# Two buffer pools in the mixer, weight sums beside the output projection, and sixteen shared feed-forward blocks instead of ten

## The chip, the core and the metric

The kernel runs on one core of one Trainium2 chip. The metric is the device time of one execution in microseconds (us). Engines are named as in the profile: PE is TensorE's matmul, PEld its weight load, DVE is VectorE, ACT is ScalarE, POOL is GpSimd, SP is SyncE, which issues nearly all transfers here.

## What is computed

One layer of a hybrid decoder on 1024 tokens of 1024 channels, all in float32. Cut to what matters here:

```python
h = rms_norm(x, norm_pre_mix)
mix = hybrid_mixer(h, ...)            # RWKV-7 heads and a causal convolution, 31 wide; then @ w_out
x = x + rms_norm(mix, norm_post_mix)
h = rms_norm(x, norm_pre_ffn)
hid = causal_dwconv(h @ ffn_up, ffn_conv_w, ffn_conv_b)   # 1024 x 5632, convolution 3 wide
gate, up = hid[..., :2816], hid[..., 2816:]
x = x + rms_norm((gelu(gate) * up) @ ffn_down, norm_post_ffn)
```

## The kernel before

**Numbers.** Each float32 operand of a large matmul is split into a high part, rounded to the matmul's format, and the rest; three matmuls (high x high, high x low, low x high) stand for one product. A weight is loaded raw (`weight`, L164), its high part is cast by ACT and its low part subtracted by POOL (`split`, L159). There are two buffers each for the parts ("wh", "wl") and three for the raw weight ("wr").

**Halves and blocks.** Tokens are worked on in two halves of 512, h0 and h1. The up projection has 22 blocks of 128 channels, each with a gate branch and an up branch. `ffn_pair` (L901) computes a block for one half: for each of two branches 8 k-tiles x 3 = 24 matmuls of 512 columns into one PSUM bank, then `taps` (L883), the convolution of three taps: one ACT pass and two DVE passes that read the bank. The product with the gelu of the gate follows on DVE.

**Plain and shared blocks.** A plain block is a pair for h0 and a pair for h1: 96 matmuls. A shared block is computed for both halves and both branches together, by Winograd's form of Strassen's product for a 2 x 2 split: seven products of 12 matmuls. Two of them need h0 alone (`gates`, L939: the first of them is copied aside as "firsts", the sum of both goes through the taps as the gate), five follow in `shared` (L1004), so 24 + 60 = 84 matmuls. The five need sums of the activations, made once (`act_sums`, L962, 3 steps for each of four k on ACT and DVE), and sums of the block's weights, made by POOL (`four_sums`, L1054, four subtractions of 128x512). The down projection (`ffn_down`, L1103) is seven such products over 11 blocks each, and sums of its weights are made ahead and kept in DRAM: `weight_sums` (L1068) has twelve steps (11 for ffn_down, one for the first shared block), each with four loads, `four_sums` and four stores.

**Numbers of blocks.** EARLY = 12 (L53), JOINT = 10 (L55), PLAIN = 22 - 10 = 12.

**Order.** The mixer works in four quarters of 256 tokens; the recurrence goes through chunks of 64. At its end (`mixer`, L1386 and on) twelve pairs of h0 (blocks 0 to 11) fill TensorE beside the last recurrence and convolution, in two "pb" banks; their results go to DRAM (`early`). Then comes the output projection of the second half (`w_out`, L763: 16 weights, 384 matmuls of 256 columns), whose six-deep weight buffers are the tags "ca" and "ck". After it `run` (L1201) opens the pools of the feed-forward part: all of the mixer's buffers lie in one pool, `mix`, that ends with it. The ten gate blocks (12 to 21) follow; `side` (L915, `beside`) puts steps of the second half's norm and then of the weight sums beside them. Then twelve pairs of h1 (blocks 0 to 11) with one step of the weight sums and one or two of `act_sums` each, then the ten shared blocks, then the down projection. From the gates on, the up projection has six banks in turn (xs, pe, pb, two each).

Instructions of an engine run in a fixed order, which the compiler's scheduler makes from priorities and its own model of time; `high_priority` and `issue_after` bend it.

## Time and profile before

| | |
|---|---|
| median of 3 runs | 1273.73 us (1272.41 to 1276.63) |
| the profiled execution | 1273.13 us |
| its span, first to last instruction | 1271.4 us |
| PE, DVE, ACT, POOL busy | 96%, 70%, 58%, 39% |
| DMA | 146 GB/s over the span, 185.7 MB |

The page has the busy time of each engine, the span in 40 slices and the chain of waits; the trace behind it can be asked for stretches, lines and tiles. The spacing of matmuls that follow each other, and not the time that one takes from start to end, says what PE can do. Stages of this kernel, by the first matmuls that belong to them: mixer to about 668 us, output projection of the second half and gate blocks to 777, pairs of h1 to 911, shared blocks to 1054, down projection to the end.

### The profile page before, as it was taken

To read this page: it belongs to the slowest core of one execution; us is meant where nothing else is said; L and a number is where in the kernel's file an instruction comes from. 1 tells how busy PE (TensorE), PEld (TensorE's weight loads), DVE (VectorE), ACT (ScalarE), POOL (GpSimd) and SP (SyncE) were. 2 spreads that over 40 slices of the span, in tenths; PEclk is the share of its full clock that TensorE was granted. 3 is DMA by queue.
4 is the path that set the end of the run, shared out by engine and by line. 5 is a ranking of instruction groups with operands and counts; after the bars stand their busy time and mean duration, and the time that the engine had idled before them with its cause. 6 is when DMAs were issued, how large, how long until landed. Compare 5 with 4: busy or idle time off the path is not lost.

```text
span 1271.4 us, 23025 instructions
## 1 busy us (share of the span) xinstructions
PE 1220.3 (96%) x8460; PEld 990.1 (78%) x8460; DVE 891.2 (70%) x1540; ACT 731.1 (58%) x1518; POOL 495.4 (39%) x438
## 2 busy tenths in 40 slices
PE   6999989999999988999999999999999999999996
PEld 4767767787778877788789878778877888888885
DVE  5286998998679989997631165666356779479667
ACT  7563563655845766566744277776555556545451
POOL 4343320011113332344455369898588860000001
PEclk9999998999999999999999999999999999999999
DMA  7644342343343451232345398888522236336523
GB/s 242 173 133 141 117 134 75 94 134 124 110 135 86 122 183 66 85 84 84 101 132 166 112 336 299 292 305 268 173 65 73 79 127 222 99 98 194 173 76 133
DMA packets 105505, 185.70 MB, mean 146 GB/s; under 512 B 15184, under 2 KB 21712, under 8 KB 105392
## 3 DMA queue, kind: packets, MB, share of 16 engines
q1 hardware_dynamic: 105392, 184.23, 46.2%
q8 instruction: 67, 1.10, 0.4%
q14 instruction: 46, 0.38, 0.1%
HBM read 141.58 MB, written 42.60 MB: 145 GB/s over the span
## 4 chain that ended last, share of the span: by engine, by line
PE 55%; DVE 8%; DMA 3%; POOL 3%; issue 2%; ACT 2%; SPq 0%; POOLq 0%; DVEq 0%; ACTq 0%
PE pb L135 26%; PE pe L135 13%; PE xs L135 11%; PE Y L135 2%; DVE pc L416 2%; PE pc L135 2%; POOL wl L162 1%; DVE nrow L1116 1%; DVE x L1100 1%; POOL b L1056 1%; PE pc L150 1%; DMA pt<-mixd 1%; DMA m<-mixd 1%; PE pe L150 0%; DMA b<-ffn_down 0%
## 5 line engine op out<-in xcount | busy, mean ns | idle before, releaser
L162 POOL TENSOR_TENSOR wl<-wr,wh 128x512 fp32r<-128x512 f32 (+1 forms) x181 | 237.2, 1312 | 247.7 <-ACT wh L162 221.0
L162 ACT CAST wh<-wr 128x512 fp32r<-128x512 f32 (+1 forms) x220 | 135.5, 616 | 170.7 <-issue 43.9
L135 PE MATMUL pb<-h,wh 128*128 128x512 f32 (+3 forms) x720 | 229.5, 398 | 2.5 <-ACT wh L162 1.0
L135 PE MATMUL pb<-f,wh 128*128 128x512 f32 x696 | 219.0, 395 | 2.6 <-ACT wh L162 1.5
L416 DVE SCALAR_TENSOR_TENSOR pc<-c,params,pc 128x512 f32<-128x512 f32 x232 | 174.1, 750 | 8.8 <-ACT pc L413 4.8
L135 PEld LDWEIGHTS pb<-h,wh 128*128 128x128 f32 (+2 forms) x720 | 131.8, 188 | 34.9 <-ACT wh L162 2.6
L135 PEld LDWEIGHTS pb<-f,wh 128*128 128x128 f32 x696 | 130.0, 189 | 31.0 <-ACT wh L162 2.8
L135 PE MATMUL pb<-h,wl 128*128 128x512 f32 (+3 forms) x360 | 146.4, 407 | 2.3 <-POOL wl L162 2.1
L135 PE MATMUL pb<-f,wl 128*128 128x512 f32 x348 | 137.9, 397 | 1.5 <-POOL wl L162 1.5
L157 POOL TENSOR_TENSOR ss<-var,mhalf 128x1 f32<-128x1 f32 x16 | 11.0, 692 | 222.6 <-DVE ss L1097 198.2
L1056 POOL TENSOR_TENSOR b<-b,b 128x512 f32<-128x512 f32 x66 | 86.8, 1317 | 2.8 <-issue 0.9
L135 PE MATMUL pe<-f,wh 128*128 128x512 f32 x272 | 84.2, 391 | 0.1
L135 PEld LDWEIGHTS pb<-h,wl 128*128 128x128 f32 (+2 forms) x360 | 67.7, 188 | 20.7 <-POOL wl L162 4.5
L135 PEld LDWEIGHTS pb<-f,wl 128*128 128x128 f32 x348 | 65.7, 189 | 16.9 <-POOL wl L162 3.1
L135 PE MATMUL xs<-f,wh 128*128 128x512 f32 x200 | 62.0, 391 | 0.4 <-DVE act L953 0.4
L135 PEld LDWEIGHTS pe<-f,wh 128*128 128x128 f32 x272 | 50.9, 188 | 10.6 <-ACT wh L162 0.3
L899 DVE SCALAR_TENSOR_TENSOR pt<-pb,params,pt 128x511 f32<-128x511 f32 (+1 forms) x48 | 35.7, 743 | 30.0 <-ACT ecarry L892 29.5
L162 POOL TENSOR_TENSOR wl<-b,wh 128x512 fp32r<-128x512 f32 x36 | 47.0, 1307 | 21.7 <-ACT wh L162 19.8
L135 PE MATMUL pe<-f,wl 128*128 128x512 f32 x136 | 53.7, 395 | 0.7 <-POOL wl L162 0.7
L706 POOL TENSOR_TENSOR XG<-r,GE 64x256 f32<-64x256 f32 x30 | 20.4, 683 | 86.9 <-DVE r L725 82.0
L178 ACT CAST wh<-wr 128x512 fp32r<-128x512 f32 (+2 forms) x44 | 26.5, 604 | 43.1 <-PE pb L135 31.2
L162 ACT CAST wh<-b 128x512 fp32r<-128x512 f32 x36 | 22.2, 617 | 46.8 <-PE pb L135 18.9
(428 smaller groups left out, 2883.7 us busy)
## 6 DMA issues: line engine op xcount, KB each, us to landing
wr<-ffn_up SPq DMA_DIRECT2D x117, 256.0 KB, 2.8
wr<-w_in SPq DMA_DIRECT2D x80, 256.0 KB, 2.9
b<-ffn_down SPq DMA_DIRECT2D x44, 256.0 KB, 4.4
sums<-b SPq DMA_DIRECT2D x44, 256.0 KB, 4.0
wr<-sums SPq DMA_DIRECT2D x44, 256.0 KB, 2.7
lows<-wl SPq DMA_DIRECT2D x40, 256.0 KB, 3.3
wl<-lows SPq DMA_DIRECT2D x40, 256.0 KB, 2.7
b<-ffn_up SPq DMA_DIRECT2D x40, 256.0 KB, 2.7
```

The source lines that it names most:

```text
L135: return self.nc.tensor.matmul(out, lhsT, rhs, start=start, stop=stop, skip_group_check=skip)
L150: self.nc.tensor.transpose(out, in_, self.con("ident")[:n, :n])
L157: self.nc.gpsimd.tensor_tensor(out, v[:, :n], self.mhalf[:, :n], ALU.pow)
L162: return self.nc.scalar.copy(hi, src), eng.tensor_tensor(lo, src, hi.bitcast(F32), ALU.subtract)
L178: self.nc.scalar.copy(hi, raw)
L416: nc.vector.scalar_tensor_tensor(out, c[:, j:j + HALF], w(j), acc, ALU.mult, ALU.add)
L706: nc.gpsimd.tensor_tensor(x[64:128], R[64:128, gs], w.GE[64:128, c, gs].unsqueeze(2).broadcast_to([64, 4, CH]), ALU.mult)
L899: nc.vector.scalar_tensor_tensor(acc[:, o:], ps[:, :HALF - o], w(j), acc[:, o:], ALU.mult, ALU.add)
L1056: sub = lambda o, x, y, op=ALU.subtract: self.nc.gpsimd.tensor_tensor(o, x, y, op)
L1100: nc.vector.scalar_tensor_tensor(x, f[c], s[:, 1:2], x, ALU.mult, ALU.add)
L1116: nc.vector.tensor_tensor(out, a, b, op)
```

## The change

JOINT becomes 16, so PLAIN is 6. EARLY stays 12: blocks 0 to 5 are plain, 6 to 11 (AHEAD = 6) are shared blocks whose gate is computed in the mixer, 12 to 21 shared blocks whose gate is computed in the gate loop as before.

- In the mixer `ahead` takes the place of `ffn_pair`: six iterations, each with the pair of plain block n and the gate of shared block 6 + n. The gate's bank takes 12 matmuls, is copied aside by ACT, waits for branch 0 of the pair (24 matmuls), takes 12 more; then comes branch 1. "firsts" and the gate go to DRAM.
- The mixer's buffers with tags l8, pt, ck, t2 and po, which the output projection uses, move to a pool of their own, `mixw`; its weights take "pt" and "ck". The feed-forward pools are put into another order, so that those that take the place of the first pool come first, and the activations' pool is cut in two (`ap`, `aq`).
- Five steps of the weight sums are put behind the 2nd, 5th, 8th, 11th and 14th weight of the output projection. With six pairs of h1, the sums are beside four of them and `act_sums` has three or two steps beside each.
- The shared blocks run in the order 6, 7, 12 to 21, 8 to 11. The gates of 6 to 11 come back from DRAM; the results of blocks 6 and 7 are stored to DRAM and come back at the end with the plain ones. `ORDER` permutes the rows of the down projection's weights to match.

```diff
-JOINT = 10
+JOINT = 16
 PLAIN = FT - JOINT
+AHEAD = EARLY - PLAIN
+STORED = 2
+ORDER = [*range(EARLY, FT), PLAIN + STORED, *range(PLAIN, PLAIN + STORED), *range(PLAIN), *range(PLAIN + STORED + 1, EARLY)]
...
+        return (self.mixw if tag in LONG else self.mix).tile(shape, dt, tag=tag, bufs=BUFS[tag], name=self.nm(tag))
...
-                wh, wl = self.weight(self.a["w_out"][ch, k2], [P, 2, 256], (self.mix, "ca", "ck") if h else None)
+                wh, wl = self.weight(self.a["w_out"][ch, k2], [P, 2, 256], (self.mixw, "pt", "ck") if h else None)
+                self.marks.append((self.load, self.low))
...
+        self.tp = pool("tp", 8)
         self.nrowp = pool("nrowp")
-        self.ap = pool("actp", 2 * JOINT)
+        self.ap = pool("actp", 15)
+        self.f2p = pool("f2p", 6)
         self.h1p = pool("h1p", 2 * KT)
-        self.tp = pool("tp", 8)
-        self.f2p = pool("f2p", 6)
+        self.aq = pool("actq", 13)
...
+    def ahead(self, hs, n, row, temp, out):
+        nc = self.nc
+        i = PLAIN + n
+        first, gate = row[:, :HALF], row[:, HALF:]
+        accs = [temp() for _ in range(2)]
+
+        def branch(br):
+            ps = self.project(self.a["ffn_up"][br * FT + n], P, hs)
+            self.taps(0, n, br, ps, accs[br])
+
+        ps = self.bank()
+        self.four(ps, self.weight(self.a["ffn_up"][i, 0], [P, 4, P]), hs[:4], True, True)
+        with self.tc.high_priority():
+            nc.scalar.copy(first, ps)
+        nc.sync.dma_start(self.firsts[n], first)
+        branch(0)
+        self.four(ps, self.weight(self.a["ffn_up"][i, 1], [P, 4, P]), hs[4:], False, True)
+        self.taps(0, i, 0, ps, gate)
+        nc.scalar.activation(gate, gate, AF.Gelu_apprx_tanh)
+        nc.sync.dma_start(self.early[i], gate)
+        branch(1)
+        nc.scalar.activation(accs[0], accs[0], AF.Gelu_apprx_tanh)
+        nc.vector.tensor_tensor(out, accs[0], accs[1], ALU.mult)
+        nc.sync.dma_start(self.early[n], out)
...
-        for n, i in enumerate(range(PLAIN, FT)):
+        for n, i in enumerate(range(EARLY, FT)):
             ps = self.bank()
...
-                late.append(self.weight(B(1, 1)(HT - HELD + len(late)), [P, 512], held=self.hp))
+                home = self.hp if len(late) < HELD - 1 else self.aq
+                late.append(self.weight(B(1, 1)(HT - HELD + len(late)), [P, 512], held=home))
...
-            one = [self.ffn_pair(0, h0, i, temp, act()) for i in range(EARLY, PLAIN)]
-            both = [[act() for _ in range(JOINT)] for _ in range(2)]
+            both = [[act(self.ap if h or n < 5 else self.aq) for n in range(FT - EARLY)] for h in range(2)]
+            for load, low in self.marks[17::3]:
+                with tc.issue_after(load.ins), tc.issue_after(low.ins):
+                    next(sums)
...
-                self.beside(sums, *[ss] * (2 if i % 3 == 0 else 1))
+                self.beside(*[sums] * (i % 3 < 2), *[ss] * (3 if i < 2 else 2))
...
+            pairs = [fetch(n) for n in range(AHEAD - STORED)]
+            order = [*range(STORED), *range(AHEAD, JOINT), *range(STORED, AHEAD)]
+            for m, n in enumerate(order):
+                two = pairs[n] if n < AHEAD else (both[0][n - AHEAD], both[1][n - AHEAD])
+                self.shared(PLAIN + n, S, h1[4:], *two, raws[m % 2 * 4:m % 2 * 4 + 4] if m else None)
+                if n < STORED:
+                    for h in range(2):
+                        nc.sync.dma_start(self.stored[h, n], two[h])
+                    pairs.append(fetch(AHEAD - STORED + n))
...
+            acts = [both[h] + [pairs[STORED][h]] + back[h] + [pairs[n][h] for n in range(STORED + 1, AHEAD)] for h in range(2)]
...
-            for i in range(EARLY):
-                if i % 2 == 0:
+            for n in range(PLAIN):
+                if n % 2 == 0:
                     two = self.row("row", 4)
-                nc.sync.dma_start(self.early[i], self.ffn_pair(0, h0, i, piece, two[:, i % 2 * HALF:(i % 2 + 1) * HALF]))
+                self.ahead(h0, n, self.row("row", 4), piece, two[:, n % 2 * HALF:(n % 2 + 1) * HALF])
```

## Rows read from the trace of the kernel before

**Rows 1.** Page: span; then busy share in tenths in 40 equal slices.

```profile
span 1271.4 us, 23025 instructions
...
PE   6999989999999988999999999999999999999996
...
DVE  5286998998679989997631165666356779479667
...
PEclk9999998999999999999999999999999999999999
```

**Rows 2.** Windows: stretch, length, busy us (instructions) by engine, granted clock, DMA share, GB/s.

```profile
497.60:632.00 134.40, 133.02 (x1234) 106.68 (x1234) 114.63 (x186) 83.15 (x173) 58.03 (x48) 0.99 0.29 85
632.00:668.30 36.30, 35.44 (x157) 29.22 (x157) 12.56 (x17) 17.50 (x35) 20.34 (x16) 1.00 0.45 126
668.30:725.50 57.20, 56.96 (x432) 54.80 (x430) 7.89 (x11) 18.28 (x49) 24.78 (x20) 1.00 0.46 135
725.50:776.70 51.20, 49.15 (x225) 39.12 (x226) 34.09 (x61) 36.82 (x84) 35.46 (x30) 1.00 0.90 313
776.70:905.00 128.30, 126.85 (x551) 102.20 (x550) 72.86 (x108) 91.14 (x193) 107.30 (x85) 1.00 0.80 269
911.00:1054.00 143.00, 141.29 (x611) 112.95 (x610) 92.80 (x134) 79.82 (x166) 111.61 (x85) 1.00 0.34 105
```

**Rows 3.** Chain that ended last, pieces: start us, us, engine, tile, line, count.

```profile
730.33 6.90 DMA m<-mixd
...
900.31 10.88 PE pb L135 x48
...
923.78 2.54 POOL b L1056 x2
```

**Rows 4.** Windows, filling matmuls alone (operand f): length, PE busy (count), PEld, DVE, ACT.

```profile
497.60:632.00 134.40, 106.19 (x422) 77.94 (x422) 0.86 (x2) 0.10 (x1) 0.99 0.29 85
632.00:668.30 36.30, 35.39 (x155) 28.83 (x154) 0.00 (x0) 0.00 (x0) 1.00 0.45 126
```

**Rows 5.** Timeline, two branches' last matmul and taps: start us, us, engine, line, operation.

```profile
574.50 0.39 PE L135 MATMUL pb<-f,wl 128*128 128x512 f32 x1
...
579.79 0.73 DVE L899 SCALAR_TENSOR_TENSOR pt<-pb,params,pt 128x510 f32<-128x510 f32 x1
...
651.54 0.39 PE L135 MATMUL pb<-f,wl 128*128 128x512 f32 x1
...
653.17 1.53 DVE L899 SCALAR_TENSOR_TENSOR pt<-pb,params,pt 128x511 f32<-128x511 f32 x2 [3.18 <-ACT ecarry L892]
```

**Rows 6.** Timeline, DVE: the last splits of the convolution's result.

```profile
629.36 2.50 DVE L162 TENSOR_TENSOR l<-co,l 128x512 fp32r<-128x512 f32 x4 [0.56 <-ACT l L162]
```

**Rows 7.** Lines of ACT, 776 to 905: count, busy us, mean ns, idle before.

```profile
L162 ACT CAST wh<-wr 128x512 fp32r<-128x512 f32 x46 | 28.6, 622 | 29.5 <-PE xs L135 7.0 <-PE pb L135 5.7 <-issue 5.0
L896 ACT ACTIVATE acc<-ecarry,acc,params 128x1 f32<-128x1 f32 x66 | 21.8, 384 | 0.3
L890 ACT ACTIVATE acc<-pe,params 128x512 f32<-128x512 f32 x8 | 6.2, 780 | 0.0
...
L910 ACT ACTIVATE xs<-acc 128x512 f32<-128x512 f32 x5 | 3.0, 601 | 0.3 <-DVE acc L899 0.3
L977 ACT COPY Y<-f 128x512 f32<-128x512 f32 x4 | 2.4, 590 | 0.0
```

**Rows 8.** Lines of POOL: 660 to 725.6 (wm, wl), then 776 to 905 (b).

```profile
L162 POOL TENSOR_TENSOR wm<-wr,wm 128x512 fp32r<-128x512 f32 x16 | 20.7, 1292 | 13.6 <-ACT wm L162 12.7 <-PE pb L135 0.6
L162 POOL TENSOR_TENSOR wl<-wr,wh 128x512 fp32r<-128x512 f32 x8 | 10.4, 1302 | 14.6 <-ACT wh L162 14.6
...
L1056 POOL TENSOR_TENSOR b<-b,b 128x512 f32<-128x512 f32 x39 | 50.5, 1294 | 1.9 <-issue 0.9
```

**Rows 9.** Windows of 10 us: a stretch of the tail, clock third from the end.

```profile
510.00:520.00 10.00, 9.95 (x185) 7.84 (x179) 9.79 (x15) 6.09 (x10) 3.49 (x3) 0.83 0.12 41
```

**Rows 10.** Windows of 10 us: a stretch of the norm, DMA share and GB/s last.

```profile
730.00:740.00 10.00, 10.00 (x46) 8.25 (x45) 7.12 (x12) 5.07 (x12) 3.58 (x4) 1.00 0.99 354
```

More of the change, by code (lines that the diff above doesn't have):

```diff
@@ L105, in __init__ @@
         self.low_pool = True
+        self.tags = {}
+        self.marks = []
     def nm(self, s):
@@ L123, in tl @@
     def tl(self, tag, shape, dt=F32):
-        return self.mix.tile(shape, dt, tag=tag, bufs=BUFS[tag], name=self.nm(tag))
+        return (self.mixw if tag in LONG else self.mix).tile(shape, dt, tag=tag, bufs=BUFS[tag], name=self.nm(tag))
     def par(self, name, j, n=P):
@@ L167, in weight @@
         with self.tc.high_priority():
-            raw = (self.f2p.tile(shape, F32, tag="f2", name=self.nm("wr")) if held is self.hp else
+            raw = (self.f2p.tile(shape, F32, tag="f2", name=self.nm("wr")) if held and held is not self.h1p else
                    self.wp.tile(shape, F32, tag="wr", bufs=3, name=self.nm("wr")))
@@ L207, in setup @@
         self.early = self.dp.tile([EARLY, P, HALF], F32, name="early")
+        self.firsts = self.dp.tile([AHEAD, P, HALF], F32, name="firsts")
+        self.stored = self.dp.tile([2, STORED, P, HALF], F32, name="stored")
         self.x1d = self.dp.tile([SEQ, D], F32, name="x1d")
@@ L220, in setup_mixer @@
         self.mix = pool("mix")
+        self.mixw = pool("mixw")
         self.banks = {"pb": 2, "pc": 1, "pe": 2}
@@ L281, in pair @@
     def pair(self, what, pool):
-        return tuple(pool.tile([P, HALF], F32R, tag="h", name=self.nm(what)) for _ in range(2))
+        return tuple(pool.tile([P, HALF], F32R, tag=self.tags.get(pool, "h"), name=self.nm(what)) for _ in range(2))
     def pairs(self, what, pool=None):
@@ L1070, in weight_sums @@
         nc, a = self.nc, self.a
-        work = [(lambda r, c, j=j: a["ffn_down"][c, r * HT + j], lambda n, j=j: self.sums[n - 1, j]) for j in range(HT)]
+        work = [(lambda r, c, j=j: a["ffn_down"][c, ORDER[r * HT + j]], lambda n, j=j: self.sums[n - 1, j]) for j in range(HT)]
         work.insert(2, (lambda r, c: a["ffn_up"][c * FT + PLAIN, r].rearrange("p k m -> p (k m)"),
@@ L1107, in ffn_down @@
         A11, A12, A21, A22 = acts[0][:HT], acts[0][HT:], acts[1][:HT], acts[1][HT:]
[L1108 removed]
+        B = lambda r, c: lambda j: self.a["ffn_down"][c, ORDER[r * HT + j]]
         T = lambda n: lambda j: self.sums[n - 1, j]
@@ L1207, in run @@
             h0 = self.mixer(sts)
+        tc = self.tc
         with ExitStack() as ctx:
@@ L1229, in run, with fetch @@
             raws = [self.h1p.tile([P, HALF], F32, tag="h", name=self.nm("b")) for _ in range(8)]
-            for n, i in enumerate(range(PLAIN, FT)):
-                self.shared(i, S, h1[4:], both[0][n], both[1][n], raws[n % 2 * 4:n % 2 * 4 + 4] if n else None)
-            kept = []
-            for i in range(0, 8, 2):
-                two = self.row("row", 4)
-                nc.sync.dma_start(two.rearrange("p (i t) -> p i t", i=2), self.early[i:i + 2].rearrange("i p t -> p i t"))
-                kept += [two[:, :HALF], two[:, HALF:]]
-            back = [self.hp.tile([P, HALF], F32, tag="h", name=self.nm("act")) for _ in range(2 * KT)]
-            for i in range(8, EARLY):
-                nc.sync.dma_start(back[PLAIN + i - 8], self.early[i])
-            for i in range(PLAIN):
-                nc.sync.dma_start(back[i], self.plain[i])
-            acts = [kept + back[PLAIN:] + one + both[0], back[:PLAIN] + both[1]]
+            def fetch(n):
+                pair = act(), act()
+                nc.sync.dma_start(pair[0], self.early[PLAIN + n])
+                nc.sync.dma_start(pair[1], self.firsts[n])
+                return pair
+            pairs = [fetch(n) for n in range(AHEAD - STORED)]
[7 more added lines that the diff above has]
+                    pairs.append(fetch(AHEAD - STORED + n))
+            back = [[self.hp.tile([P, HALF], F32, tag="h", name=self.nm("act")) for _ in range(STORED + PLAIN)] for _ in range(2)]
+            for k in range(STORED + PLAIN):
+                for h in range(2):
+                    src = self.stored[h, k] if k < STORED else (self.plain if h else self.early)[k - STORED]
+                    nc.sync.dma_start(back[h][k], src)
+            acts = [both[h] + [pairs[STORED][h]] + back[h] + [pairs[n][h] for n in range(STORED + 1, AHEAD)] for h in range(2)]
             self.ffn_down(acts)
```

5 lines of the change are left out of this document (3 added, 2 removed).

## Prediction

> **What bounds the kernel now.** I read the page first: TensorE is busy nearly everywhere and at the high granted clock in almost every slice, while VectorE is full only in the first half [rows 1]. A mean over stages with different limits says little of a change in some of them, so next I cut the span into the six stages that the edit touches and set the time of each against its matmul work [rows 2]. The unit for that comes from the chain of waits, where 48 matmuls of 512 columns follow each other in 10.88 us [rows 3], that is 0.2267 us each (the "mean ns of one" of a matmul is its latency, not its spacing).
>
> Stage by stage, with the stretches of [rows 2]:
> - 497.6 to 632 (tail of the mixer, feed-forward pairs as filling). 422 filling matmuls [rows 4] are 422 x 0.2267 = 95.7 us of 134.4. The other 38.7 us are the recurrence's and the convolution's small matmuls and the bubbles between them. VectorE is busy 114.6 of 134.4: it and the chain of the recurrence set this pace. The convolution's last split ends at 629.36 + 2.50 = 631.9 [rows 6].
> - 632 to 668.3 is nothing but the rest of the filling: 155 matmuls, 35.1 of 36.3 us [rows 4]. TensorE alone bounds it; VectorE does 12.6 us.
> - 668.3 to 725.5, output projection with the first gate blocks in between: PE 57.0 of 57.2.
> - 725.5 to 776.7, rest of the gate blocks and the norm of the second half: PE idles 2.0 us (51.2 - 49.15), DMA at 0.90; the chain goes here through a 6.9 us load of the norm [rows 3].
> - 776.7 to 911, twelve pairs of the second half: 576 x 0.2267 = 130.6 us of 134.3, 3.7 lost, POOL at 107.3 of 128.3 to 905.
> - 911 to 1054, ten shared blocks: 600 x 0.2267 = 136.0 of 143, 7 lost, most of it in one place at 923 where POOL's weight sums of the second block are late [rows 3].
>
> So from 632 on TensorE is the bound, and a matmul taken away there is time taken away; before 632 it is so only as far as others don't set the pace.
>
> **The change, part by part.** The sum is made against the profiled execution, 1273.1 us (span 1271.4); the median shown is 1273.7, 0.6 more.
>
> (1) Matmuls. A plain block costs 48 for each half, 96; a shared one 24 (gate) + 60 = 84. Six blocks change sides: 6 x 12 = 72 matmuls fewer, 72 x 0.2267 = **-16.3 us**. But they come off as three terms at different places. In the mixer 6 x 72 = 432 instead of 12 x 48 = 576: -144, -32.6 us. In the second half's pairs 6 instead of 12: -288, -65.3 us. In the shared blocks 16 instead of 10: +360, +81.6 us. The 240 of the gate loop stay.
>
> (2) Is the -32.6 us of the mixer really to be had? Up to 632 the old order got 422 filling matmuls done; the new one needs 432 in all. The old rest of 36.3 us shrinks to ten matmuls, 2.3 us, if the filling runs at the old rate. VectorE's share doesn't grow (per iteration three tap pairs and one product for 72 matmuls against two and one for 48), ACT's copies of the first sums (0.6 us, six) and POOL's splits neither. What gets worse is the bank rhythm. In the mixer the filling has two "pb" banks. Before, 24 matmuls on the other bank lie between a branch's end and the next use of its bank, 5.44 us. In `ahead` the gate block holds one bank across branch(0), so branch(1), and the next branch(0), find only 12 in between: 2.72 us. The lag from a branch's last matmul to the end of its second tap is 579.79 + 0.73 - 574.89 = 5.6 us where VectorE is full and 653.17 + 1.53 - 651.93 = 2.8 us where it is free [rows 5]. There are 12 such places. If nothing else is put into the gap, they cost 12 x (5.6 - 2.7) = 35 us at the one and 1 us at the other. But 38.7 us of other PE work has to go somewhere in this stage, 3.2 us for each place, about the 2.9 us that is missing. So most of the wait is not new time. I take **+4 us**, between 0 and +20 (a gain is excluded: less than no wait there is not). Behind the waiting matmuls stand, in PE's order, those of the recurrence, for which VectorE and ACT then wait.
>
> A rule of the skill speaks against this part. The rows show the granted clock at 1.00 from 668 on, where six banks are in turn [rows 2], and 0.83, part of it at the lower level, in a ten-microsecond stretch of the tail, where two are and PE was just filling gaps between small matmuls [rows 9]. The Trainium skill, "TensorE: Matmul & The Clock Gate", section "A second HAM failure mode: psum-queue depth-cycling", says that cycling through banks with small idles between the groups makes the clock fall and rise again. By the rows the sum gets nothing for it; by the rule it would be a rival, (E) below.
>
> (3) Weight sums at the output projection. Five of the twelve sums (marks 17, 20, 23, 26, 29) now run there: each four loads and four stores of 256 KB on SP, and four POOL operations of 1.294 us, 5.2 us [rows 8]. That is 25.9 us of POOL and 10.5 MB. POOL has there 16 splits of w_out and 8 of gate blocks, 20.7 + 10.4 = 31.1 us [rows 8]; together 57.0 of the 57.2 us that PE takes. So POOL is just not the bound, as long as its order lets the splits go first. DMA moves 135 GB/s there [rows 2]; 10.5 MB over 57.2 us are 184 more, 319, under the 354 GB/s that the trace reached [rows 10]. In return the next stage, with DMA at 0.90 and the norm's loads on the chain, has fewer sums to load, and its buffers are there before the output projection ends. On SP the stores of a sum wait for POOL, and queued behind them are the loads of w_out and later of the norm. Bounds: -4 (the 2.0 us idle and the wait for the norm's load go) to +6 us (one SP wait like the 6.9 us load of [rows 3], not hidden). I take **0**.
>
> (4) Six instead of twelve pairs for the second half, with the same act_sums beside. Here ACT is the thing to count. A pair costs it 4 casts x 0.622 + 2 x 0.780 + 6 one-column activations x 0.384 + one gelu 0.601 = 6.95 us; act_sums are 11 operations for each of four k at about 0.59, 26 us [rows 7]. Before: 12 x 6.95 + 26 = 109 us under 130.6 us of PE. After: 6 x 6.95 + 26 = 67.7 us under 65.3. ACT becomes the bound of this stage by 2.4 us, and a cast of a weight then comes late, with POOL's split and 12 matmuls behind it. POOL gets easier: 6 x 4 x 1.29 + 4 sums x 5.2 = 52 us. The stage lost 3.7 us before and should lose about 5 now: **+1.5 us**, bounds -2 (no loss beyond the 2.4 us of ACT) to +7 (ACT's surplus and one more wait like that at 923 in a row).
>
> (5) Six more shared blocks beyond their matmuls. The loss at 923 is at the entry, and stays: the raw weights' buffers come free only after the last pair. The rest of the stage lost about 3 us in nine blocks, 0.3 a block: with the two blocks that are stored and the fetches by SP, **+1.2 us**, bounds 0 to +4.
>
> (6) Down projection: the activations that come back from DRAM are now needed from its third product on, no more from its first; the held weights' buffers come free one by one in the fifth product. PE is saturated there, and nothing shown waits: 0. New stores and loads of "firsts" (6 and 6, 256 KB) and "stored" (4 and 4) are 5.2 MB among 185.7: 0, hidden under the shared blocks, where DMA is at 0.34 [rows 2].
>
> Sum: -16.3 + 4 + 0 + 1.5 + 1.2 = -9.6 us; 1273.1 - 9.6 = 1263.5, with the 0.6 between profile and median **1264 us**.
>
> **The rivals.**
> (A) the forecast, 1258 to 1270.
> (B) All of the matmul term and some of the old losses too: bank waits hidden entirely (0), stage 725.5 to 776.7 and the pairs at their lower bounds (-4, -2), +0.6: -21.7, near 1252; I put 1253 for it. For it: a lighter DMA load just where the norm is on the chain. Against: ACT in the pairs.
> (C) The gain is eaten after 668: POOL at 57.0 of 57.2 and ACT at 67.7 of 65.3 each turn into waits at their upper bounds (+6, +7), with +4 for the banks: -16.3 + 4 + 6 + 7 + 1.2 = +1.9, with half of the two bounds 1269; call it 1272 (1270 to 1277). For it: both counts are at their limit. Against: weights are asked for with high priority, and six of w_out's fit ahead.
> (D) Slower: the bank wait in `ahead`. If the recurrence's matmuls don't fall into the gaps (PE's order is fixed beforehand, and the lag on the chip is what VectorE makes of it), each of the places pays lag - 2.72. The other terms are -13.6, so it is slower by over 3.8 us from 17.4 / 12 + 2.72 = 4.2 us of mean unhidden lag on; the rows have 5.6 and 2.8. With the larger lag at eight of the twelve, before VectorE gets free, 8 x 2.9 = 23 us: 1273.7 - 13.6 + 23 = 1283. Against: 3.2 us of other PE work for each place.
> (E) The clock falls with the bank waits. A ten-microsecond stretch at 0.83 loses 1.7 us; at each of the 12 places that is 20 us, on top of (A) 1284. Only one stretch of the tail shows it so far. The Trainium skill's section named above is what speaks for it.
> (F) The change doesn't do what it says: the new buffers, though in a pool of their own, wait for something that ends late (the last of the mixer's tiles, or SP's queue), and the sums slip behind the output projection. Then ten of them meet six pairs: POOL 6 x 4 x 1.29 + 10 x 5.2 = 83 us under 65.3, +17.7, less the 5 already counted in part: near 1278.
>
> **How the numbers follow.** A measurement of this kernel can tell a change of about 0.3%, 3.8 us, from none; so faster is under 1269.9, slower over 1277.5. Chances: A 0.46, B 0.17, C 0.16, D 0.12, E 0.02, F 0.07. Faster: B and nearly all of A, 0.62. Within: C, a little of A and half of F, 0.21. Slower: D, E and half of F, 0.17. The likeliest is A, 1264 us. The range must leave out no more than 0.2: it starts at 1251, where some of B is still below, and ends at 1279, which leaves out most of D and E.
>
> **What would show it.** The output projection starts near 636 instead of 666 if (2) holds, and the count of filling matmuls before 632 is over 400; PE then waits for VectorE's taps in the tail by less than 5 us in all. Under (D) the output projection starts after 650 and the waits of PE for the taps add up to over 15 us. POOL between 636 and 695 over 90% busy with sums and no wait of PE for it over 2 us supports (3); under (F) no sum operation is seen before the output projection's end. In the pairs ACT over 90% busy and PE losing about 5 us supports (4). Sixteen shared blocks at 13.6 to 13.9 us each support (5). The prediction is wrong if the tail's end moves by less than 20 us, or if a stage between the output projection and the first shared block loses over 8 us more than now.

## The result, and where the time came from

The changed kernel takes 1280.61 us (median of 12 runs, 1275.76 to 1284.39) against 1274.97 for the kernel before on the same chip: a ratio of 1.0047, 95% interval 1.003 to 1.0063. It was forecast to be 10 us faster, and is 6 us slower. Its profiled execution took 1279.6 us with a span of 1277.8, 6.4 more than the span before.

The page of the changed kernel, the rows that answer [rows 1]:

```profile
span 1277.8 us, 22909 instructions
...
PE   5989989999999989999999999989999999999996
...
PEclk8999998999999999999999899999999999999998
```

Nothing stands out at this scale, except some clock digits of 8 where the kernel before has 9, one of them in the middle of the span (703 to 735 us). So the stages again, as windows from one stage's first matmul to the next one's (columns as in [rows 2]): the mixer's tail up to the convolution's last split, the rest of the filling, the output projection, the gates up to the norm's last transpose, the pairs, the shared blocks.

```profile
497.20:634.40 137.20, 133.96 (x1232) 106.81 (x1233) 111.04 (x183) 84.69 (x178) 56.46 (x48) 0.99 0.33 99
634.40:640.20 5.80, 3.27 (x14) 2.05 (x12) 2.05 (x4) 4.12 (x9) 1.16 (x1) 1.00 0.77 238
640.20:694.80 54.60, 53.92 (x410) 52.51 (x411) 8.02 (x12) 17.72 (x47) 48.05 (x38) 0.97 0.93 304
694.80:754.20 59.40, 56.52 (x250) 45.47 (x249) 32.52 (x57) 37.95 (x84) 36.79 (x33) 0.94 0.82 278
754.20:826.90 72.70, 67.40 (x290) 53.34 (x289) 46.52 (x73) 54.84 (x116) 56.23 (x45) 1.00 0.81 273
826.90:1058.20 231.30, 225.01 (x962) 178.84 (x961) 149.01 (x219) 126.04 (x266) 183.59 (x140) 0.99 0.31 93
```

Read at the same first matmuls, before and after (us; output projection and gates as one, because gate matmuls lie in both):

| stage | before | forecast | after | off by |
|---|---|---|---|---|
| tail, filling to first w_out matmul | 170.4 | 141.8 | 143.0 | +1.2 |
| output projection and gates | 108.4 | 108.4 | 113.9 | +5.5 |
| pairs of h1 | 134.6 | 70.8 | 72.6 | +1.8 |
| shared blocks | 140.9 | 223.7 | 231.3 | +7.6 |
| down projection to the last matmul | 209.5 | 209.5 | 209.7 | +0.2 |

So the 72 matmuls are gone, and 23 us of new losses stand against their 16.3. Three handovers from one stage to the next show where much of it begins. The timeline shows each (start us, us, engine, line, operation, then the idle time before it and what ended it):

```profile
638.84 0.76 ACT L903 ACTIVATE pt<-pb,params 128x512 f32<-128x512 f32 x1
639.54 1.66 ACT L170 CAST wm<-wr 128x512 fp32r<-128x512 f32 x3
640.22 0.39 PE L143 MATMUL pb<-wm,l 128*128 128x256 f32 x1 [2.04 <-ACT wm L170]
641.27 6.94 PE L143 MATMUL pb<-wm,l 128*128 128x256 f32 x42 [0.67 <-DVE pt L912]
...
698.70 0.38 SPq L801 DMA_DIRECT2D mixd<-t  x1
702.91 1.75 SPq L878 DMA_DIRECT2D m<-mixd  x4
705.93 3.11 DVE L879 SCALAR_TENSOR_TENSOR nrow<-m,nr,nrow 128x512 f32<-128x512 f32 x3 [4.82 <-DMA m<-mixd]
711.12 0.63 ACT L986 ACTIVATE act<-act 128x512 f32<-128x512 f32 x1 [4.81 <-DVE act L912]
713.53 0.77 PE L143 MATMUL pe<-f,wh 128*128 128x512 f32 x2 [2.26 <-ACT wh L170]
713.55 1.28 POOL L170 TENSOR_TENSOR wl<-wr,wh 128x512 fp32r<-128x512 f32 x1 [5.72 <-ACT wh L170]
...
829.46 0.59 ACT L1021 COPY r<-Y 128x512 f32<-128x512 f32 x1 [1.89 <-DVE s L170]
831.84 0.58 ACT L170 CAST f<-pe 128x512 fp32r<-128x512 f32 x1
832.87 0.62 ACT L170 CAST wh<-wr 128x512 fp32r<-128x512 f32 x1
833.57 2.53 POOL L170 TENSOR_TENSOR wl<-wr,wh 128x512 fp32r<-128x512 f32 x2 [4.61 <-ACT wh L170]
836.06 2.54 POOL L1095 TENSOR_TENSOR t<-b,b 128x512 f32<-128x512 f32 x2
...
847.78 0.79 PE L143 MATMUL pe<-s,wl 128*128 128x512 f32 x1 [2.26 <-POOL wl L170]
```

and of the kernel before the first cast of a w_out weight and the last cast of the activation sums:

```profile
661.89 0.62 ACT L162 CAST wm<-wr 128x512 fp32r<-128x512 f32 x1 [1.33 <-DMA wr<-w_out]
...
884.63 0.57 ACT L162 CAST f<-pb 128x512 fp32r<-128x512 f32 x1
```

- **Start of the output projection, 640.** The first cast of a w_out weight runs on ACT only behind the tap pass of the last filling pair; TensorE waits 2.0 us for it. Before, 36 us of filling lay here, and the first of these casts ran at 661.89, 6 us ahead of its matmul.
- **The norm, 694 to 715.** One chain through every engine: the norm's rows come by DMA, VectorE waits 4.8 us for them with the gates' taps queued behind, ACT's gelu waits for a tap with the weight casts behind it, POOL's split waits for a cast, TensorE 2.3 us for the cast and 0.6 for the split.
- **Entry of the shared blocks, 827 to 850.** The last of the activation sums are still on ACT at 829 to 832, a weight cast stands behind them, POOL waits 4.6 us for it, and the weight sums of the second shared block, which are behind it on POOL, start 9.2 us after the first shared product. TensorE waits for ACT and POOL five times here, 2.3 us at the longest. In the kernel before the first of these sums starts 4.8 us after the first shared product, and the last cast of the activation sums ran at 884.63, 26 us ahead of the entry at 911.

A fourth wait lies between the norm and the pairs: TensorE waits 2.1 us for the split of the first pair's weight, which stands behind two weight sums on POOL (timeline of the changed kernel):

```profile
752.75 2.52 POOL L1095 TENSOR_TENSOR b<-b,b 128x512 f32<-128x512 f32 x2 [2.63 <-issue]
755.22 1.28 POOL L170 TENSOR_TENSOR wl<-wr,wh 128x512 fp32r<-128x512 f32 x1
...
756.55 0.50 PE L143 MATMUL pb<-f,wl 128*128 128x512 f32 x1 [2.07 <-POOL wl L170]
```

The three handovers cost a second time, through the clock. Windows around the three (clock third from the end), a stretch and what TensorE did just before it:

```profile
640.00:642.40 2.40, 1.52 (x9) 1.21 (x10) 1.99 (x3) 1.20 (x3) 2.16 (x2) 1.00 0.30 116
642.40:645.80 3.40, 3.40 (x19) 3.40 (x18) 0.00 (x0) 0.62 (x1) 3.40 (x4) 0.50 0.88 186
711.00:714.10 3.10, 0.84 (x4) 0.30 (x2) 2.26 (x6) 2.98 (x8) 0.55 (x1) 1.00 1.04 418
714.10:720.90 6.80, 6.22 (x16) 4.80 (x16) 3.55 (x7) 5.38 (x13) 4.04 (x5) 0.50 0.96 370
840.00:847.20 7.20, 4.47 (x17) 2.58 (x15) 5.28 (x8) 5.30 (x12) 7.20 (x6) 1.00 0.00 1
847.20:850.60 3.40, 2.82 (x7) 2.24 (x8) 1.72 (x3) 0.60 (x1) 3.01 (x3) 0.50 0.69 199
```

After each of these pauses the granted clock is at 1.2 instead of 2.4 GHz for 3.4 or 6.8 us. TensorE was busy 3.40 + 6.22 + 2.82 = 12.4 us there. Half of that, about 6 us, is an estimate of what the low clock cost; it holds if nothing but TensorE set the pace there. The kernel before shows 1.00 in every stretch of [rows 2] from 632 to 1054. The Trainium skill, "TensorE: Matmul & The Clock Gate", section "HAM oscillation — how this bites in real kernels", describes a kernel that pays its waits again behind them, at a lower clock, with waits of 3 to 5 us for a DMA. These rows agree that a wait can be paid again; but no single wait here is over 2.3 us.

A pause alone doesn't settle it. Behind the wait at 756 the clock stayed at 1.00. And a kernel of the next section, a_order, has the last of the three pauses once more, with the same wait of 2.3 us, and stays at the high level behind it:

```profile
838.20:845.40 7.20, 4.52 (x18) 2.63 (x16) 5.23 (x8) 5.30 (x12) 7.20 (x6) 1.00 0.00 0
845.40:848.80 3.40, 2.75 (x12) 2.29 (x13) 1.93 (x4) 0.92 (x2) 3.09 (x3) 1.00 0.66 205
```

Its first 120 matmuls of the shared blocks lose 6.6 us against their spacing of 0.2267, those of the changed kernel 7.9: the low clock was worth 1.3 us there, near the half of 2.82. What decides whether the clock falls behind such a pause is not shown.

### The profile page after: what moved, and what is told of

It reads as the page before. It is cut to its first block, busy times and chain, and to the rows that moved or that the text cites. A ratio compares the mean times of both kernels' runs of the same rounds, so it can differ in the third digit from the quotient of the medians.

```text
span 1277.8 us, 22909 instructions
## 1 busy us (share of the span) xinstructions
PE 1211.5 (95%) x8388; PEld 978.5 (77%) x8388; DVE 906.1 (71%) x1570; ACT 728.4 (57%) x1516; POOL 517.4 (40%) x456
## 4 chain that ended last, share of the span: by engine, by line
PE 51%; DVE 10%; POOL 4%; ACT 3%; issue 2%; DMA 2%; SPq 0%; POOLq 0%; DVEq 0%; ACTq 0%
PE pb L143 21%; PE pe L143 13%; PE xs L143 12%; POOL wl L170 2%; DVE pc L427 2%; PE Y L143 2%; PE pc L143 2%; DVE nrow L1155 1%; DVE x L1139 1%; DMA b<-ffn_down 1%; POOL b L1095 1%; DVE sub L602 1%; DMA sums<-b 1%; ACT wh L170 0%; DVE dw L604 0%
## 5 line engine op out<-in xcount | busy, mean ns | idle before, releaser
L170 POOL TENSOR_TENSOR wl<-wr,wh 128x512 fp32r<-128x512 f32 (+1 forms) x145 | 189.1, 1305 | 222.6 <-ACT wh L170 193.4
L143 PE MATMUL pb<-f,wh 128*128 128x512 f32 x592 | 187.0, 396 | 2.5 <-DVE pt L912 1.9
L170 ACT CAST wh<-wr 128x512 fp32r<-128x512 f32 (+1 forms) x184 | 113.0, 615 | 119.7 <-PE pb L143 34.6
L143 PEld LDWEIGHTS pb<-f,wh 128*128 128x128 f32 x592 | 110.5, 189 | 26.1 <-issue 2.0
L143 PE MATMUL pb<-f,wl 128*128 128x512 f32 x296 | 117.7, 398 | 2.9 <-POOL wl L170 2.9
L1095 POOL TENSOR_TENSOR b<-b,b 128x512 f32<-128x512 f32 x78 | 105.5, 1354 | 5.9 <-issue 2.6
L170 POOL TENSOR_TENSOR wl<-b,wh 128x512 fp32r<-128x512 f32 x60 | 78.1, 1302 | 34.0 <-ACT wh L170 34.0
L170 ACT CAST wh<-b 128x512 fp32r<-128x512 f32 x60 | 37.0, 617 | 80.1 <-PE pb L143 29.6
L170 DVE TENSOR_TENSOR a<-act,a 128x512 fp32r<-128x512 f32 x66 | 44.8, 698 | 22.9 <-ACT a L170 20.6
L170 ACT CAST a<-act 128x512 fp32r<-128x512 f32 x66 | 39.4, 618 | 37.2 <-PE Y L143 20.6
```

The costliest lines, as they stand in the source:

```text
L143: return self.nc.tensor.matmul(out, lhsT, rhs, start=start, stop=stop, skip_group_check=skip)
L170: return self.nc.scalar.copy(hi, src), eng.tensor_tensor(lo, src, hi.bitcast(F32), ALU.subtract)
L1095: sub = lambda o, x, y, op=ALU.subtract: self.nc.gpsimd.tensor_tensor(o, x, y, op)
```

## The experiments

Stages of the kernels that follow, in us, read as above (the last transpose and some gate matmuls change places, so the sum up to the first shared product is the safer column; a kernel without activation sums has only the sum of the last two; in a_relief_four ten matmuls of the last pair come behind the first shared product, so its last column is the one to read):

| kernel | tail | w_out, gates | pairs | sum to here | shared | pairs + shared |
|---|---|---|---|---|---|---|
| before | 170.4 | 108.4 | 134.6 | 413.4 | 140.9 | 275.5 |
| after | 143.0 | 113.9 | 72.6 | 329.5 | 231.3 | 303.9 |
| a_nosums | 143.0 | 112.7 | 69.5 | 325.2 | 231.1 | 300.6 |
| b_nosums | 168.8 | 108.4 | 131.0 | 408.2 | 141.1 | 272.1 |
| a_noact | 143.0 | 112.6 | | | | 296.8 |
| b_noact | 170.4 | 112.6 | | | | 275.0 |
| a_order | 142.6 | 111.7 | 73.2 | 327.5 | 230.3 | 303.5 |
| j14 | 154.4 | 116.7 | 93.1 | 364.2 | 197.4 | 290.5 |
| a_relief | 143.0 | 113.8 | 72.3 | 329.1 | 227.2 | 299.5 |
| b_relief | 170.4 | 108.4 | 136.1 | 414.9 | 141.7 | 277.8 |
| a_four | 142.7 | 113.3 | 72.7 | 328.7 | 227.4 | 300.1 |
| a_relief_four | 143.0 | 112.5 | 71.3 | 326.8 | 230.1 | 301.4 |
| a_ca | 141.6 | 109.0 | 76.0 | 326.6 | 230.6 | 306.6 |
| a_relief_ca | 140.9 | 106.4 | 74.5 | 321.8 | 226.5 | 301.0 |

### Is it the weight sums?

Both kernels without the sums of the weights (a_ from the changed kernel, b_ from the one before); plain weights of the same size stand in for them:

```diff
-        for src, dst in work:
-            ...
+        for _ in range(HT + 1):
+            yield
```

> The changed kernel without the weight sums: no loads, subtractions and stores of sums, neither beside the output projection nor later; the down projection and the first shared block load plain weights of the same size in their place. To be set against b_nosums. Theory 1: the gain was eaten after the output projection's start by two things, the sums' transfers and POOL work (about 5.6 us in the gate stage, where the norm's loads come late) and ScalarE in the six pairs (about 8 us up to the second shared block). Then this kernel is 5 to 8 us faster than b_nosums, because the sums' part is gone and ScalarE's remains; about 1262 us. Rival 2: the sums are all of it; then it is 11 us or more faster than b_nosums (16.3 of matmuls less 5.1 in the mixer's tail). Rival 3: neither, something in the shared blocks; then it is no faster than b_nosums.

> The kernel before, with the same left out: no weight sums, plain weights of the same size instead. All theories: a few us faster than the kernel before, 3 to 7 us, as its gate stage and pairs lost about 6 us beside the sums; about 1268 us. It gives the ground for a_nosums.

Measured against before: a_nosums 1.0016 (1.0 to 1.0032), b_nosums 0.9962 (0.9946 to 0.9978). Each kernel gains, and the distance between them stays: 0.54% instead of 0.47%. The sums cost 3 us of pairs and shared blocks in either. They are not what ate the gain in the changed kernel.

### Is it ACT? Two tries

The first: the edge columns of h1's taps (three one-column operations each) moved from ACT to two on VectorE, in both kernels.

```diff
-                for c, k, j in ((0, 1, 1), (0, 0, 0), (1, 1, 0)):
-                    a = acc[:, c:c + 1]
-                    nc.scalar.activation(a, carry[:, k:k + 1], AF.Identity, scale=w(j), bias=a)
+                for n, k, j in ((1, 1, 1), (2, 0, 0)):
+                    a = acc[:, :n]
+                    nc.vector.scalar_tensor_tensor(a, carry[:, k:k + n], w(j), a, ALU.mult, ALU.add)
```

> The changed kernel with one thing taken off ScalarE: the three one-column activations at the left edge of each branch of the second half (0.38 us each, six for a pair and six for a shared block) become two small VectorE operations. ScalarE loses 2.3 us for each pair, 13.8 us in the six pairs, and comes from 67.7 to 54 us under 65.3 us of matmuls. Theory 1: the loss in the pairs and at the entry of the shared blocks goes, 6 to 8 us: about 1273 us. Rival 2 (weight sums are all of it): within 2 us of the changed kernel, about 1280. Rival 3 (shared blocks themselves): ScalarE is lighter there too, so 2 to 4 us, from blocks and not from the pairs.

> The kernel before with the same edit of the edge columns. ScalarE has there 109 us under 130.6 us of matmuls in the pairs, so theory 1 expects little: 0 to 2 us, about 1273. If it gains as much as a_edges does, ScalarE wasn't the difference between the two kernels.

Measured: 1.0226 (1.0201 to 1.0252) and 1.0161 (1.0137 to 1.0185), a clear miss. Lines of VectorE in a_edges, 780 to 1058 (count, busy us, mean ns of one):

```profile
L1087 DVE TENSOR_TENSOR act<-act,acc 128x512 f32<-128x512 f32 x14 | 24.5, 1748 | 0.0
L909 DVE SCALAR_TENSOR_TENSOR acc<-fcarry,params,acc 128x2 f32<-128x2 f32 x10 | 13.1, 1308 | 0.0
...
L909 DVE SCALAR_TENSOR_TENSOR acc<-ecarry,params,acc 128x1 f32<-128x1 f32 x14 | 8.6, 614 | 6.3 <-ACT ecarry L905 6.3
```

and one such operation of its timeline while POOL ran nothing:

```profile
826.44 0.20 DVE L909 SCALAR_TENSOR_TENSOR acc<-ecarry,params,acc 128x2 f32<-128x2 f32 x1
```

In these groups one or two columns take 0.6 to 1.3 us, at the most nearly twice a whole tap's 0.75. All have two inputs in SBUF, and POOL is busy with sums from SBUF most of that time (207 of the 278 us). The ten of them in a_edges during which POOL ran nothing took 0.20 to 0.22 us. The Trainium skill, "SBUF — State Buffer", section "Who interferes with whom", has the rule: such an operation and a POOL operation that reads SBUF exclude each other for a whole instruction; the rows agree with it. So the edit made VectorE wait for POOL, and says nothing of ACT.

The second: the activation sums left out altogether, parts of h0 standing in for them.

```diff
         for k in range(4):
-            a11, a12, a21, a22 = h0[k], h0[4 + k], h1[k], h1[4 + k]
-            ...
+            for n, p in ((1, h0[k]), (2, h0[k]), (3, h0[4 + k]), (4, h0[4 + k])):
+                S[n].append(p)
+                if n < 4:
+                    yield
```

> The changed kernel without the activation sums for the shared blocks: no copies, additions and splits of act_sums; parts of the first half's activations stand in their place as operands. To be set against b_noact. The runs without weight sums left the distance between the two kernels at 8 us, so the weight sums are not what ate the gain. Theory 1b: it is ScalarE, into whose six pairs all of act_sums is now pressed (67.7 us of work under 65.3 us of matmuls), with the entry of the shared blocks behind it, 8 us together. Then this kernel is level with b_noact or a little faster (0 to 4 us), and 8 to 12 us faster than the changed kernel, about 1270 us. Rival 4: the pairs' loss comes from elsewhere (bank rhythm, buffers); then it stays 5 us or more slower than b_noact.

> The kernel before with the same left out. Theory 1b: ScalarE had room in the twelve pairs, so 1 to 4 us faster than the kernel before, about 1272 us. It gives the ground for a_noact.

Measured: a_noact 0.9992 (0.9974 to 1.001), b_noact 1.0029 (1.001 to 1.0047). Pairs and shared blocks as one window, in the changed kernel and in a_noact:

```profile
754.20:1058.20 304.00, 292.41 (x1250) 232.18 (x1249) 195.53 (x291) 180.88 (x381) 239.82 (x184) 0.99 0.43 136
```

```profile
752.70:1049.50 296.80, 291.96 (x1249) 232.31 (x1248) 167.27 (x243) 161.35 (x339) 240.22 (x184) 0.99 0.44 141
```

The same work costs 7 us in the changed kernel and half a microsecond before (275.5 against 275.0), where twelve pairs lie over it. That b_noact is slower than before was not expected: it starts its filling 2 us later and loses 4 us in the output projection and gates, which the edit doesn't touch; its clock is at the lower level for 3.4 us from 633 and again from 674, where the kernel before has none. Such shifts of other stages, by the order that the scheduler makes, are why the stages are compared and not the totals alone.

This leaves open what of the activation sums does it: ACT, VectorE or the banks that they hold. So one line moves their twelve copies from ACT to VectorE:

```diff
                 r = self.f2p.tile([P, HALF], F32, tag="f2", name=self.nm("r"))
-                nc.scalar.copy(r, src)
+                nc.vector.tensor_copy(r, src)
```

> The changed kernel with one line of the activation sums edited: their twelve copies of 128x512 out of a bank are made by VectorE instead of ACT. ACT loses 12 x 0.585 = 7.0 us and a hop to ACT and back for each copy, VectorE gets 12 x 0.69 = 8.3 us more (46.5 of the 72.7 us of the six pairs are busy there). Theory (the activation sums press on ACT's order: weight casts stand behind them, in the pairs and at the entry of the shared blocks): pairs and shared blocks together 303.9 -> about 300, time 1276 to 1279. Rival (it is the banks that the activation sums hold, or VectorE): not faster than 1281, up to 1284.

> The same edit in the kernel before. There the activation sums have twelve pairs to lie beside, and leaving them out altogether changed pairs and shared blocks from 275.5 to 275.0 us. Theory: nothing, 1274 to 1276, pairs and shared blocks 275 to 276. Rival (copies on VectorE help wherever they are): 2 to 4 us faster, 1271 to 1273.

Measured: a_relief 1.0003 (0.9991 to 1.0015), b_relief 0.9997 (0.9978 to 1.0015), as the theory of ACT's order has it. (b_relief's profile has 277.8 instead of 275.5 us for pairs and shared blocks, so the copies on VectorE are no help there.) In a_relief every stage is that of the changed kernel but one: the shared blocks take 227.2 instead of 231.3. Its windows of the pairs and of the first 30 us of the shared blocks:

```profile
754.20:826.50 72.30, 67.29 (x290) 53.26 (x289) 56.01 (x88) 50.54 (x110) 56.71 (x45) 1.00 0.81 277
826.50:856.50 30.00, 27.59 (x117) 21.25 (x116) 16.98 (x26) 14.08 (x29) 24.02 (x19) 1.00 0.45 151
```

and its timeline, the first weight sum of the second shared block:

```profile
832.71 1.29 POOL L1095 TENSOR_TENSOR t<-b,b 128x512 f32<-128x512 f32 x1
```

It starts 6.2 instead of 9.2 us after the first shared product, the stretch of low clock at 847 is gone, and 117 instead of 99 matmuls are done in those 30 us. The pairs themselves didn't move: there ACT wasn't the bound (54.84 busy of 72.70 in the changed kernel). What counts is the tail of the activation sums on ACT at the entry, with weight casts behind it. The edit also saves each copy the way to ACT and back; it doesn't tell the two apart.

### Is it the banks in the mixer?

The gate block's two halves next to each other, so that its bank isn't held across a branch:

```diff
         nc.sync.dma_start(self.firsts[n], first)
-        branch(0)
         self.four(ps, self.weight(self.a["ffn_up"][i, 1], [P, 4, P]), hs[4:], False, True)
         self.taps(0, i, 0, ps, gate)
         nc.scalar.activation(gate, gate, AF.Gelu_apprx_tanh)
         nc.sync.dma_start(self.early[i], gate)
+        branch(0)
         branch(1)
```

> The changed kernel with one thing changed in the mixer's filling: both halves of the gate block directly behind each other, then the two branches of the pair. Each branch then has 24 matmuls on the other bank before its bank is needed again, as in the kernel before; instead PE waits once in each iteration for the copy of the first sums (0.6 us and the signals, about 1 us). Theory: the tail of the mixer, 143 us in the changed kernel where 138 were left by the matmuls, loses 2 to 4 us less; about 1277 us in all. Rival: the tail is set by VectorE and the recurrence; then it stays at 143 us and the time is that of the changed kernel within 2 us.

Measured: 1.005 (1.0032 to 1.0068), the tail 142.6 instead of 143.0; the 2 to 4 us of the theory didn't come. TensorE's waits for the taps in the tail are 1.9 us in all in the changed kernel and 1.8 here, so it isn't the exchange of banks that makes them. Nor does TensorE wait for the copy of the first sums in the new order, as was expected. What the bank rhythm costs there is too little to measure.

### Fourteen shared blocks

```diff
-JOINT = 16
+JOINT = 14
-STORED = 2
+STORED = 0
```

(with the loops fitted to it: four of the mixer's eight fillings are plain pairs.)

> Fourteen shared blocks instead of sixteen: eight plain ones, four gates made in the mixer (its other four iterations are plain pairs), no stored blocks; the rest as in the changed kernel. 24 matmuls more than the changed kernel, 48 fewer than the kernel before (10.9 us). In the pairs ScalarE has 8 x 6.95 + 26 = 81.6 us under 87.1 us of matmuls. Theory 1b: the loss in the pairs and at the entry falls from 11 to about 5 us, that of the bank places (eight for twelve) by a third: 1271 to 1275 us, 5 to 9 us faster than the changed kernel though it has 5.4 us more matmuls. Rival 4: losses as in the changed kernel, so 5 us slower than it, about 1285.

Measured: 1.0043 (1.0024 to 1.0061), a miss. The pairs keep a loss of 6 us over their 384 x 0.2267 = 87.1, and the entry loses less (2.5 us in the first 120 matmuls instead of 7.9). But the output projection loses more: 59.1 us with the same 26 gate matmuls that take 54.5 in the changed kernel. The wait at its start is there again, and shorter; what costs more is one in its middle, for a gate block's weight whose load landed late, and the clock behind it (timeline, then a window of j14):

```profile
653.70 0.39 PE L143 MATMUL pb<-wm,l 128*128 128x256 f32 x1 [1.44 <-ACT wm L170]
...
699.84 0.62 ACT L170 CAST wh<-wr 128x512 fp32r<-128x512 f32 x1 [2.81 <-DMA wr<-ffn_up]
700.51 0.74 PE L143 MATMUL xs<-f,wh 128*128 128x512 f32 x2 [4.05 <-ACT wh L170]
```

```profile
701.70:705.10 3.40, 3.40 (x19) 3.40 (x18) 0.00 (x0) 0.62 (x1) 1.86 (x3) 0.50 1.05 381
```

That load was issued at 694.4, among the loads and stores of the weight sums, and took 5.4 us. This is the danger that part (3) of the prediction priced; it came true here and not in the changed kernel.

### Is it SP's order at the norm?

The fifth weight sum at the output projection, whose stores stand on SP ahead of the store that the norm waits for, slips to later:

```diff
-            for load, low in self.marks[17::3]:
+            for load, low in self.marks[17:27:3]:
```

> The changed kernel with four instead of five weight sums at the output projection; the last one there, behind the 14th weight, slips to later places. Its stores stood on SP ahead of the store that the norm waits for. Theory (SP's order makes the norm late): that store is issued about 1 us after the last matmul of the output projection instead of 4, the stretch from there to the norm's last transpose goes from 59.4 to about 56, the time to 1277 to 1279. Rival (the norm is late by its own loads and by the weights that six more gate blocks ask for there): stretch 59 to 60, time 1280 to 1283, as the sum costs elsewhere what it cost here.

> Both edits together in the changed kernel. If each is worth what its theory says, 3 to 4 us at the shared blocks and 3 at the norm, they lie in different stretches and add up: 1273 to 1276, level with the kernel before. Rivals: only one of them works, 1277 to 1280; neither, 1281.

Measured: a_four 1.0025 (1.0012 to 1.0039), a_relief_four 1.0014 (1.0002 to 1.0026). The store did move (SP's queue in a_four, where the output projection's last matmul is at 701.9):

```profile
702.91 0.38 SPq L801 DMA_DIRECT2D mixd<-t  x1
```

That is 1.0 us behind instead of 3.9. But output projection and gates went from 113.9 to 113.3 only: SP's order wasn't what made the norm late, and that theory falls. a_four's 3 us came at the entry of the shared blocks (227.4), the place that a_relief mends, and the two don't add up (pairs and shared blocks 300.1, 299.5, and 301.4 with both). In a_four the last copy of the activation sums runs 0.6 instead of 2.6 us after the first shared product and the first weight sum 6.5 instead of 9.2, so the same tail on ACT is shorter there; what made it so was not tested.

### Is it the buffers of w_out's weights?

The change gives the high parts of these weights the buffers "pt", which the filling pairs use for their taps, instead of "ca", free since the convolution. Back again:

```diff
-LONG = "l8", "pt", "ck", "t2", "po"
+LONG = "l8", "ca", "ck", "t2", "po"
...
-                wh, wl = self.weight(self.a["w_out"][ch, k2], [P, 2, 256], (self.mixw, "pt", "ck") if h else None)
+                wh, wl = self.weight(self.a["w_out"][ch, k2], [P, 2, 256], (self.mixw, "ca", "ck") if h else None)
```

> The changed kernel with the two tags swapped back for the weights of w_out: tag ca instead of pt lies in the second pool and takes their high parts, as in the kernel before; pt, the filling pairs' temporaries, stays in the first pool. Theory (the casts wait for buffers that the last pairs still hold): the first cast comes before the last tap passes, TensorE's 2.0 us wait and the stretch of low clock at 642 behind it (1.4 us) go, the output projection starts near 638 and loses under 0.5 us instead of 2.8; 3 us faster, 1276 to 1279. Rival (ACT's order puts the cast behind the passes of the last pair whatever buffer it has): start at 640, loss 2.5 to 3, time 1280 to 1282.

> The same with the twelve copies of the activation sums on VectorE. Theory of independent losses: 4 us at the entry of the shared blocks and 3 at the start of the output projection, about 1271 to 1273, a little faster than the kernel before. Rival (the buffers change nothing): 1274 to 1276 as with the copies alone.

Measured: a_ca 0.9999 (0.9986 to 1.0012); a_relief_ca 0.9962 (0.9949 to 0.9976), 1269.6 us, **faster than both kernels**. The first is level with the kernel before, not faster. In a_ca the first cast comes at 632.8 instead of 639.5 (timeline):

```profile
632.81 0.64 ACT L170 CAST wm<-wr 128x512 fp32r<-128x512 f32 x1
...
640.43 5.75 PE L143 MATMUL pb<-wm,l 128*128 128x256 f32 x46
```

No wait stands before the first matmul of the output projection, and 46 follow each other in 5.75 us, where the changed kernel's 42 took 6.94 after a wait. The timed gain, 0.5% or 6 us, is more than the 3 expected; a_ca's profiled execution, 1277.7, lay above its median of 1274.0 and shows only a part of it: 2.9 us up to the first shared product. Where the rest lies is not shown. a_relief_ca's stages, as windows:

```profile
498.00:638.90 140.90, 135.87 (x1244) 107.68 (x1245) 114.30 (x185) 88.51 (x185) 59.78 (x50) 1.00 0.33 100
638.90:698.90 60.00, 59.90 (x443) 57.24 (x444) 9.71 (x14) 19.61 (x52) 49.98 (x41) 1.00 0.93 316
698.90:745.30 46.40, 43.42 (x202) 34.30 (x201) 30.09 (x55) 33.67 (x76) 31.47 (x27) 1.00 0.91 313
745.30:819.80 74.50, 69.94 (x303) 55.95 (x302) 55.40 (x88) 52.78 (x110) 58.37 (x46) 1.00 0.80 274
819.80:1046.30 226.50, 223.03 (x961) 177.99 (x960) 151.33 (x218) 124.90 (x263) 183.62 (x139) 1.00 0.31 94
```

The clock is at 1.00 in all of them, though one wait of 2.1 us, at the first pair, is still there. Two edits of one or two lines that take no matmul away bring the changed kernel from 6 us over the old one to 5 below it. The weight sums stand at the output projection as before, with POOL at 49.98 of 60.00 there. So about 11 of the 23 us lost were spent at two handovers and can be had back; the other 12 are still lost in this kernel.

## Why the prediction was wrong, step by step

(1) **Matmuls: right.** The down projection and the count of matmuls are as worked out.

(2) **The tail: right in size, for another reason.** 420 filling matmuls were done before the convolution's last split, 422 before [rows 4]:

```profile
497.20:634.40 137.20, 106.51 (x420) 77.60 (x421) 0.88 (x2) 0.04 (x1) 0.99 0.33 99
```

The cost was 5.2 us for a forecast of 4. But a_order has nearly the same tail without the bank rhythm: 2 us are the wait for w_out's first cast, 0.5 one for a split, and the split of the convolution ends 2.5 us later than before. TensorE's waits for taps are 1.9 us in all, under the 5 named as a sign. Rival (D) is out. That the number came near is luck.

(3) **Sums at the output projection: forecast 0, measured +5.5, near the bound of +6.** The priced danger, POOL and SP, wasn't it: POOL was busy 48.05 of the projection's 54.60 and TensorE waited for it nowhere there, and a_nosums has nearly the same 112.7 without any sum. What the step left out is a line of the diff that looked like bookkeeping: the weights' new buffers. They make the first casts wait for the filling pairs just when the filling no longer hides it. With the old ring the same stage takes 109.0 and 106.4. Some of that comes back in the pairs (76.0 and 74.5 instead of 72.6); by the sum up to the first shared product the ring is worth 2.9 us, by the medians 6. The other part of the loss is the norm's handover, a wait of 2.3 us and 6.8 us of low clock; no edit took it away alone, and what started it stays open.

(4) **Pairs: forecast +1.5, measured +3.3, inside its bounds, by luck.** The working was wrong. ACT was not over 90% busy but 75% (54.84 of 72.70). Its operations that follow each other overlap: the single durations in this stage add up to 63.6 us (three one-column ones in a row take 0.94 us, not the 3 x 0.384 of [rows 7]). Some of the count ran only later, at the entry of the shared blocks. Taking 7 us from ACT left the stage as it was. 2.1 of the 3.3 us are the wait at 756, behind weight sums on POOL; without the sums the pairs took 69.5 us, not 72.6.

(5) **Shared blocks: forecast +1.2, bounds 0 to +4, measured 231.3 - 140.9 - 81.6 = +8.8, or 14.5 us a block.** This is the step that failed outright. "The loss at 923 is at the entry, and stays": it didn't stay. The first 120 matmuls lose 7.9 us instead of 2.9, because the activation sums, over twelve pairs done 26 us before the entry, now end inside it. What step (4) took for ACT's surplus in the pairs came one stage later, in an in-order queue, as late weight casts. 4 us of the entry's loss are shown by a_relief. The rest of these blocks lost 0.4 us a block instead of 0.2, in a_nosums too; that stays open. (The stage before ended at 1051.9, not at 1054: it had lost 4.9 us, not 7.)

(6) **Down projection: right**, 209.7 against 209.5.

Of the rivals, (C), the gain eaten after 668, came nearest in kind and had 0.16. It named POOL and ACT as engines that become full; no engine was full. (E)'s mechanism was there, but behind waits at handovers and not in the bank rhythm: the stretches of low clock cost an estimated 6 us. A forecast that prices a wait by its length alone leaves that out.

## What to carry to other kernels

When work is taken out of a stage that covered a handover, go through what the cover hid: which buffers the next stage's first loads and casts take, who held them last, and what stands ahead of them in each in-order queue. Side work that had room over twelve steps must end before the next stage when it has six; count when its last operation runs, not only how busy its engine is. And a wait of TensorE of two microseconds can be paid again behind it if the clock falls, as it did three times here and didn't at the same pause in a_order; so look at the granted clock after each new wait.

## What the runs showed of the hardware

- In the changed kernel the granted clock fell to its lower level for 3.4 to 6.8 us after pauses in which no single wait of TensorE exceeded 2.3 us, with TensorE at 0.84 of 3.10, 1.52 of 2.40 and 4.47 of 7.20 us just before. In a_order it stayed at the high level behind 4.52 of 7.20 us with the same wait. In a_relief_ca, with the first and the last of the three gone and one wait of 2.1 us left, it was at the high level from 498 to 1046.
- VectorE operations of one or two columns with both inputs in SBUF took 0.20 to 0.22 us while POOL ran nothing and up to 1.3 us beside it (a_edges), and a 128x512 product of two SBUF tiles 1.75 us, where the tap of 511 columns that reads a bank stays near 0.74.
- Twelve copies of 128x512 out of banks cost VectorE 0.68 us each (a_relief), and the kernel before no time that its median shows (b_relief, 0.9997).
